# A hybrid encoder block on one core: attention's values taken one chunk later, and one list of other work over all pairs of heads

## The chip, the cores and the metric

The kernel runs on one core of a Trainium2 chip. The metric is device time in microseconds of one execution; shorter is better. A core has TensorE (PE; PEld is its weight load), VectorE (DVE), ScalarE (ACT), GpSimd (POOL) and SyncE (SP, which here issues nearly all DMAs). Each engine works through its own list of instructions in a fixed order and waits for others on semaphores.

## What is computed

One layer of an encoder block on 1024 positions of width 1024, with 16 learned meta positions put ahead (1040 in all). After an RMS norm, one input projection feeds two branches:

```
z = u @ w_in                          # u = RMSNorm(h)
rq, rk, rv, rg, aq, ak, av, ag, gr, ga = split(z)
branch A: bidirectional retention (4 heads), group norm, times silu(rg), @ w_rb
branch B: windowed attention (8 heads, 2 key groups), times silu(ag), @ w_ab
out = h + RMSNorm((sigmoid(gr) * A + sigmoid(ga) * B) @ w_o)
```

The attention works on blocks of 128 queries. A block sees its own 128 keys, those of the block before and the block after (within 128 positions), and the 16 meta keys; each head has a sink logit that takes part in the softmax:

```
s = concat(q . k_band, q . k_meta) * scale, masked
p = exp(s - m) / (sum(exp(s - m)) + exp(sink - m))
o = p_band @ v_band + p_meta @ v_meta
```

## The kernel before

All products are made to nearly full precision out of three rounded ones: each operand is split into a rounded high part (a copy, on ScalarE or GpSimd) and a low part (a subtraction on VectorE), and mm3 (lines 71 to 76) issues high x high, low x high and high x low. So every operand of a matmul costs a copy and a subtraction before TensorE can use it.

The stages follow each other. First the retention for four heads (lines 444 to 616), each with a forward and a backward scan over eight chunks; in the backward scan projections of the next head are put between the steps. After the fourth head come the projection of the attention's values (gen_av, lines 1246 to 1259, tile pav, copied to vraw) and the attention (lines 1261 to 1417). Then four large products, z, r, a and o (lines 1232 to 1237), run as seven products of blocks instead of eight; for these, sums of rows of x are made ahead (sum_fetch and sum_row, lines 689 to 705: load 2 x 512 KB, scale on ScalarE, four subtractions on VectorE, store to device memory), and some of the products of z too (gen_pre, lines 755 to 777, tile pe).

The attention handles pairs of heads hp = 0 to 3, with 8 chunks n of 128 queries each: 32 chunks. Pairs 0 and 1 use key group 0, pairs 2 and 3 group 1. A chunk has three stages:

- stage1 (lines 1274 to 1322): the scores of both heads (tile ps, three matmuls each), on VectorE the masked scores and their least value (raw, nm), on ScalarE the exponential with its sum (p, den), on VectorE the reciprocal, on GpSimd the scaling of p. It splits what it needs if that is not there yet: the queries (split_q, lines 635 to 641, tiles aqh and aql, from aq) and the values (vsplit, lines 1265 to 1272).
- stage2 (lines 1324 to 1356): TensorE transposes p into two banks (tile pt), ScalarE and VectorE split the result into pah and pal, pm, pbh and pbl.
- stage3 (lines 1358 to 1373): TensorE multiplies with the values (tile po, 7 or 10 matmuls), ScalarE copies to oa, and every second chunk SP stores oa.

The order is written out by hand in the loop of lines 1389 to 1417. For a chunk k it is: stage1 of k+1, stage2 of k, some steps of other work, stage3 of k. `follow` holds instructions behind those that it names, so that each engine's order comes out as written. The other work is a generator; one step is three matmuls, and FILL (line 26) says how many steps go into each chunk. It consists of projections of later queries (gen_aq, tile paq), keys of group 1 (gen_ak, tile pak) and early products of z (pe). Each pair of heads has its own list (fills, lines 1425 to 1433), and a new one begins when the pair ends. The weights for it (load_w, tiles wr, wh, wl; pre_fetch and pre_parts, tiles we, weh, wel) are loaded into two buffers of 512 KB that all loads share with the row sums; load_w issues the load and both splits together, with the high part on GpSimd. Keys of group 1 need the buffers of group 0, so between the pairs 1 and 2 the order is different: 16 steps ahead of the values of chunk (1, 7), and 16 more after the scores of (2, 0).

The row sums are made in the retention, one k for each head (lines 547 to 550). Three copies of rows of x to the output (x_to_out, lines 1419 to 1423) are issued after the first pair.

Of the kernel before, what the change touches and what calls it, by code (L numbers as in the profile page):

```python
# [25 lines left out]
FILL = (6, 5, 5, 5, 5, 5, 4, 5), (6, 5, 5, 6, 6, 6, 6, 16), (6, 5, 5, 5, 5, 5, 4, 5), (7, 7, 7, 7, 6, 6, 8)  # L26
# [12 lines left out]
def block_kernel(ctx: ExitStack, tc: tile.TileContext, xT, x, w_in, w_rb, w_ab, w_out, vecs, dec, sink,  # L39
# [62 lines left out]
    def load_w(src, u, act=False):  # L102
        hi, lo = [], []
        for s in range(2):
            raw = keep.tile([P, 4, 256], F32, tag="wr", bufs=2, name=f"wr{u}_{s}")
            nc.sync.dma_start(raw, src[u, :, 4 * s:4 * s + 4, :])
            h = wp.tile([P, 4, 256], R, tag="wh", bufs=4, name=f"wh{u}_{s}")
            l = wp.tile([P, 4, 256], R, tag="wl", bufs=4, name=f"wl{u}_{s}")
            if act:
                nc.scalar.copy(h, raw)  # L110
            else:
                pool_hi(h, raw)
            dve_lo(l, raw, h)
            hi.append(h)
            lo.append(l)
        return (lambda k, a, b: hi[k // 4][:, k % 4, a:b]), (lambda k, a, b: lo[k // 4][:, k % 4, a:b])

# [301 lines left out]
    vraw = va.tile([P, NB, 256], F32, name="vraw")  # L419
# [24 lines left out]
    def retention(h, fill):  # L444
# [199 lines left out]
    def load_aq(hp):  # L644
        wq[hp] = load_w(w_in, U_AQ + hp)

    def gen_aq(hp, i):
        if not i:
            if hp not in wq:
                load_aq(hp)  # L650
            aq[hp] = {}
        a, b = HALVES[i]
        for e_ in range(2):
# [4 lines left out]
            if hp or i:  # L658
                split_q(hp, e_, i)
# [5 lines left out]
    def load_ak():  # L665
        wak.append(load_w(w_in, U_AK))

    def gen_ak(g):
        if not wak:
            load_ak()  # L670
        kh, kl = (ra.tile([P, 4, 272], R, tag="kp", bufs=2, name=f"kT{s}{g}") for s in "hl")
        kT[g] = (kh, kl)
        for i, (a, b) in enumerate(PIECES):
            t = yield from proj(wak[0], P * g, a, b, f"pak{g}_{i}")
            o = ra.tile([P, 272], F32, tag="ak", bufs=2, name=f"akr{g}_{i}")
            rope_evac(t, a, b, o, f"ak{g}_{i}")
            s = NM if i == 0 else 0
            nc.scalar.copy(kh[:, i, 0:256], o[:, s:s + 256])
            dve_lo(kl[:, i, 0:256], o[:, s:s + 256], kh[:, i, 0:256])
            if i == 0:  # L680
                for j in range(4):
                    nc.scalar.copy(kh[:, j, 256:272], o[:, 0:NM])
                    dve_lo(kl[:, j, 256:272], o[:, 0:NM], kh[:, j, 256:272])
            yield
# [53 lines left out]
    def pre_parts(u):  # L738
# [4 lines left out]
        with follow(*softmax[-1:]):  # L743
            if n > P:
                v = t[:, :, P:n]
                g(v, raw[0][:, :, P:n], v, ALU.add)
                g(v, v, raw[0][:, :, 0:P], ALU.subtract)
                g(v, t[:, :, 0:P], v, ALU.subtract)
            h = wp.tile([P, 4, 256], R, tag="wh", bufs=4, name=f"weh{u}")[:, :, 0:n]
            l = wp.tile([P, 4, 256], R, tag="wl", bufs=4, name=f"wel{u}")[:, :, 0:n]  # L750
            nc.scalar.copy(h, t[:, :, 0:n])
            dve_lo(l, t[:, :, 0:n], h)
        parts[u] = h, l

    def gen_pre(u):
# [5 lines left out]
        ahead = 9 < u < 13  # L761
        if ahead:
            pre_fetch(u + 1)
        for p in PRE[u]:
# [10 lines left out]
            if ahead and p == 2:  # L775
                pre_parts(u + 1)
            yield

    def hooked(gen, at):

        for n, _ in enumerate(gen):
            for f, *a in at.get(n, ()):
                f(*a)
            yield
# [11 lines left out]
    scored, softmax, stored, values = [], [], [], {}  # L796
# [29 lines left out]
    last = "o", 3, 4  # L826
# [13 lines left out]
    class Phase:  # L840
# [65 lines left out]
        def product(self, u, p):  # L906
            if (self.nm, u, p) == last:
                return self.last_product(u, p)
            st = self.u.setdefault(u, {})
            at = {1: "X", 6: "X", 7: "W" if u in self.apart else "X", 5: "Y", 3: "V" if u in self.early or (self.nm, u) == last[:2] else "Y", 2: "Z",  # L910
# [26 lines left out]
        def combine(self, u, p, st):  # L937
# [28 lines left out]
            elif p == 6:  # L966
                copy("u2")
                if (self.nm, u) == last[:2]:
# [8 lines left out]
            elif p == 7 and not apart:  # L977
                copy("u3")
                if (self.nm, u) == last[:2]:
                    done("X")  # L980
            elif p == 3 and (self.nm, u) == last[:2]:
# [11 lines left out]
            if "u3" in st and "Y" in st and "c22" not in st:  # L993
                st["c22"] = plus(new("c5") if (self.nm, u) == last[:2] else st["u3"], st["u3"], "Y")
                self.post(u, 1, 1, st["c22"])
                if early or 3 in self.pre.get(u, ()) or (self.nm, u) == last[:2]:
# [246 lines left out]
    pm = [ap.tile([P, 256], R, name=f"pm{i}") for i in range(2)]  # L1243
    for t in (vm, pm[0], pm[1]):
        nc.vector.memset(t.bitcast(F32), 0.0)
    def gen_av():
        w = load_w(w_in, U_AV)
        for c in range(9):
# [7 lines left out]
            else:  # L1256
                nc.scalar.activation(vraw[:, c - 1], t[:, 0:256], AF.Copy, scale=rcol[:, c:c + 1])
            if c == NB - 1:
                yield

    def attention():
        oa, raw = [None], {}
        st1, st2 = {}, {}

        def vsplit(hp, b):
            g = hp // 2
            a_ = ap.tile([P, P], R, tag="vh", bufs=NB, name=f"vh{hp}_{b}")
            b_ = ap.tile([P, P], R, tag="vl", bufs=NB, name=f"vl{hp}_{b}")
            s = vraw[:, b, P * g:P * g + P]
            nc.scalar.copy(a_, s)  # L1270
            dve_lo(b_, s, a_)
            values[g, b] = (a_, b_)

        def stage1(hp, n):
# [14 lines left out]
            for b, _ in blocks:  # L1289
                if (g, b) not in values:  # L1290
                    vsplit(hp, b)
# [4 lines left out]
            for e_ in range(2):  # L1296
# [5 lines left out]
                scored.append(mm3(s[:, 0:wid], a_, b_, kh[:, start:start + wid], kl[:, start:start + wid], True, True))  # L1302
# [3 lines left out]
                p = ap.tile([P, 401], F32, tag="p", bufs=4, name=f"p{hd}_{n}")  # L1306
# [17 lines left out]
        def stage2(hp, n):  # L1324
# [33 lines left out]
        def stage3(hp, n):  # L1358
# [3 lines left out]
            for j, (b, h_, l_) in enumerate(bl):  # L1362
                mm3(po[:, 0:256], *values[g, b], h_, l_, j == 0, False)
# [13 lines left out]
        last = {}  # L1377

        def marks(*names):
            return [last[m] for m in names if m in last]  # L1380

        chunks = [(hp, n) for hp in range(4) for n in range(NB)]
        fill = filler(fills(0))[0]
        av = gen_av()
        next(av)
        stage1(0, 0)
        with follow(*latest):
            next(av, None)
        for (hp, n), follows in zip(chunks, chunks[1:] + [None]):
            if follows and follows != (2, 0):  # L1390
                with follow(*latest, *marks("oa", "lo")):
                    stage1(*follows)
            if (hp, n) == (3, NB - 2):
# [4 lines left out]
            with follow(*latest, *marks("exp", "sum")) if (hp, n) < (3, NB - 2) else ExitStack():  # L1398
                stage2(hp, n)
            if (hp, n) < (3, NB - 2):  # L1400
                if (hp, n) == (1, NB - 1):
                    fill = filler(fills(2))[0]
                with follow(*latest):
                    fill(FILL[hp][n])
            else:
                yield
            with follow(*latest) if (hp, n) < (3, NB - 2) else ExitStack():
                stage3(hp, n)
            if follows == (2, 0):
                with follow(*latest, *marks("oa", "lo")):  # L1410
                    stage1(2, 0)
                with follow(*latest):
                    fill(2 * KT)
            elif n == NB - 1 and hp < 3:
                fill = filler(fills(hp + 1))[0]
            if (hp, n) == (0, NB - 1):
                x_to_out()

    def x_to_out():

        with tc.issue_after(stored[0]):
            for r in (0, 4, 6):
                nc.sync.dma_start(out[P * r:P * r + 2 * P], x[P * r:P * r + 2 * P])

    def fills(hp):

        if hp == 1:
            return [hooked(gen_aq(1, 1), {5: [(pre_fetch, 8)], 11: [(pre_parts, 8)], 15: [(load_aq, 2)]}), pieces(pre, 8),
                    hooked(gen_aq(2, 0), {5: [(load_ak,)]})]
        if hp == 3:  # L1430
            return [hooked(gen_aq(3, 1), {3: [(pre_fetch, 10)], 9: [(pre_parts, 10)]}), pre]
        return [*([gen_ak(1)] if hp else []), hooked(gen_aq(hp, 1), {5: [(load_aq, hp + 1)]}),
                hooked(gen_aq(hp + 1, 0), {3: [(pre_fetch, 7 + hp)], 9: [(pre_parts, 7 + hp)]}), pieces(pre, 8)]
# [104 lines left out]
```

## Time and profile before

| | |
|---|---|
| runs of the kernel | 1137.64 us median of 3 (1137.25 to 1138.17) |
| the profiled execution's own time | 1137.18 us |
| its span in the profile | 1135.34 us |
| mean granted TensorE clock | 0.982 |
| first scores of the attention | at 363.2 us |
| scores of the second chunk | at 371.7 us |
| scores of the last chunk but one | at 614.4 us |
| first product of z | at 630.3 us |

A profile line of a group or of the timeline names the line in the kernel, engine, operation, output <- inputs and shape. In the timeline the first two columns are start and duration in us; in brackets stands how long the engine had been idle before, and what it waited for. Durations of matmuls overlap, since they are pipelined: what counts is the distance from one start to the next.

### The profile page before, as it was taken

What the parts mean: (1) busy time and instruction counts of PE and PEld (TensorE: products, weight loads), DVE (VectorE), ACT (ScalarE), POOL (GpSimd) and SP (SyncE); (2) the same over time, 40 slices, a digit from 0 to 9 for tenths busy, and PEclk for the clock granted to TensorE, in tenths of its full rate; (3) what the DMA queues carried; (4) which work ended last, traced back from release to release, by engine and by line L of the source; (5) the groups of instructions that cost most, each with busy time, mean ns of one, the idle gap of its engine ahead of it and who ended that gap; (6) DMA issues with size and microseconds to landing.
All of it is one profiled execution on the core that took longest, in us unless ns stands there. A gap on an engine that the chain in (4) does not pass through costs nothing.

```text
span 1135.3 us, 17083 instructions
## 1 busy us (share of the span) xinstructions
PE 1080.5 (95%) x5939; PEld 926.6 (82%) x5939; DVE 881.0 (78%) x1797; ACT 507.1 (45%) x1126; POOL 216.4 (19%) x276
## 2 busy tenths in 40 slices
PE   8999999899898899898899999999999999999997
PEld 7898889889887778697777778788888888787786
DVE  7887786877985665676666798999889979876775
ACT  7241432513423445434546664545546636433442
POOL 3323233243242322432220000000000000020032
PEclk9999999999999999899999999999999999999999
DMA  7140321411431411401124846999982763789563
GB/s 278 38 140 29 96 82 38 140 52 52 140 111 38 158 57 41 137 23 43 56 84 157 323 167 229 334 298 365 351 304 75 255 235 119 248 192 318 183 112 75
DMA packets 82903, 175.18 MB, mean 154 GB/s; under 512 B 8784, under 2 KB 22608, under 8 KB 82000
## 3 DMA queue, kind: packets, MB, share of 16 engines
q1 hardware_dynamic: 78928, 167.51, 42.9%
q0 software_dynamic: 3456, 6.29, 3.6%
q8 instruction: 47, 0.77, 0.3%
q10 hardware_dynamic: 432, 0.28, 0.1%
q14 instruction: 40, 0.33, 0.1%
HBM read 119.52 MB, written 57.67 MB: 156 GB/s over the span
## 4 chain that ended last, share of the span: by engine, by line
PE 74%; DVE 12%; DMA 7%; issue 3%; ACT 3%; POOL 1%; SPq 0%; DVEq 0%; POOLq 0%; ACTq 0%
PE bz L73 6%; PE bz L74 6%; PE bz L75 6%; PE pv L73 2%; PE br L74 2%; PE br L75 2%; PE br L73 2%; PE pv L74 2%; PE pv L75 2%; PE bo L73 2%; PE bo L74 2%; PE bo L75 2%; PE ba L74 2%; PE ba L73 2%; PE ba L75 2%
## 5 line engine op out<-in xcount | busy, mean ns | idle before, releaser
L1161 POOL DMA_DIRECT2D mx_d<-c1a x4 | 3.7, 920 | 405.8 <-DVE c1a L1152 405.8
L73 PE MATMUL bz<-T,lhz 128*128 128x512 f32 x192 | 75.6, 396 | 0.5 <-ACT u2z L943 0.4
L73 PE MATMUL pv<-wh,big 128*128 128x256 f32 x256 | 74.4, 291 | 1.6 <-DVE m_qk L174 1.3
L74 PE MATMUL bz<-T,llz 128*128 128x512 f32 x192 | 75.7, 395 | 0.0
L75 PE MATMUL bz<-T,lhz 128*128 128x512 f32 x192 | 75.6, 394 | 0.0
L74 PE MATMUL pv<-wh,big 128*128 128x256 f32 x256 | 73.6, 287 | 0.0
L75 PE MATMUL pv<-wl,big 128*128 128x256 f32 x256 | 73.3, 286 | 0.0
L73 PE MATMUL bz<-big,lhz 128*128 128x512 f32 x176 | 69.5, 397 | 1.2 <-ACT lhz L861 1.2
L74 PE MATMUL bz<-big,llz 128*128 128x512 f32 x176 | 69.7, 396 | 0.1
L75 PE MATMUL bz<-big,lhz 128*128 128x512 f32 x176 | 69.3, 394 | 0.0
L1307 DVE CUSTOM_DVE_ANT_0 raw<-ps,mask,nsink 128x400 f32<-128x400 f32 (+1 forms) x64 | 37.0, 598 | 34.6 <-PE ps L75 34.3
L1320 POOL TENSOR_SCALAR p<-p,den 128x400 f32<-128x400 f32 (+1 forms) x60 | 38.4, 654 | 130.4 <-DVE den L1313 113.4
L1310 ACT ACTIVATE p<-raw,nm 128x401 f32<-128x401 f32 (+1 forms) x64 | 38.4, 601 | 37.7 <-DVE nm L1307 37.5
L73 PE MATMUL paq<-big,wh 128*128 128x512 f32 x128 | 52.3, 409 | 0.0
L73 PEld LDWEIGHTS pv<-wh,big 128*128 128x128 f32 x256 | 49.2, 192 | 2.5 <-DVE m_qk L174 1.5
L74 PE MATMUL paq<-big,wl 128*128 128x512 f32 x128 | 50.6, 395 | 0.0
L75 PE MATMUL paq<-big,wh 128*128 128x512 f32 x128 | 50.4, 394 | 0.0
L74 PEld LDWEIGHTS pv<-wh,big 128*128 128x128 f32 x256 | 49.3, 193 | 0.1
L75 PEld LDWEIGHTS pv<-wl,big 128*128 128x128 f32 x256 | 49.2, 192 | 0.0
L89 DVE TENSOR_TENSOR wl<-wr,wh 128x1024 fp32r<-128x1024 f32 x28 | 37.3, 1335 | 15.3 <-POOL wh L86 15.1
L73 PEld LDWEIGHTS bz<-T,lhz 128*128 128x128 f32 x192 | 36.2, 188 | 9.7 <-ACT u2z L943 1.4
L75 PEld LDWEIGHTS bz<-T,lhz 128*128 128x128 f32 x192 | 36.2, 188 | 8.5
(631 smaller groups left out, 3651.0 us busy)
## 6 DMA issues: line engine op xcount, KB each, us to landing
wrz<-in_w_in_dram SPq DMA_DIRECT2D x32, 512.0 KB, 5.7
wr<-in_w_in_dram SPq DMA_DIRECT2D x29, 512.0 KB, 3.7
e<-e SPq DMA_DIRECT2D x40, 256.0 KB, 3.8
we<-in_w_in_dram SPq DMA_DIRECT2D x16, 512.0 KB, 3.7
tg<-tg_d SPq DMA_DIRECT2D x32, 256.0 KB, 4.9
T<-preT SPq DMA_DIRECT2D x6, 1024.0 KB, 7.1
xs<-in_xT_dram SPq DMA_DIRECT2D x8, 512.0 KB, 3.5
xsT<-xs SPq DMA_DIRECT2D x16, 256.0 KB, 2.1
```

The costliest lines, as they stand in the source:

```text
L73: nc.tensor.matmul(o, ah, bh, start=first, stop=False, **kw)
L74: nc.tensor.matmul(o, al, bh, start=False, stop=False, **kw)
L75: latest[:] = [nc.tensor.matmul(o, ah, bl, start=False, stop=last, **kw).ins]
L89: return nc.vector.tensor_tensor(o, i, hi.bitcast(F32), ALU.subtract).ins
L1161: nc.gpsimd.dma_start(d, to, accum_op=ALU.add)
L1307: nc.vector.tensor_tensor_reduce(raw[e_][:, 1:1 + wid], s[:, 0:wid], mask[:, mo:mo + wid], -SCALE, nsink[:, hd:hd + 1], ALU.add, ALU.min, ...
L1310: last["exp"] = nc.scalar.activation(p[:, 0:1 + wid], raw[e_][:, 0:1 + wid], AF.Exp, scale=-1.0, bias=nm_[:, e_:e_ + 1], accum_out=den[:, ...
L1320: nc.gpsimd.tensor_scalar(pt[e_][:, 0:wid], pt[e_][:, 0:wid], den[:, e_:e_ + 1], 1.0, op0=ALU.mult, op1=ALU.mult)
```

## The change

Four things are done, all in the attention and what feeds it.

1. *Order of a chunk.* After: stage1 of k+1, stage2 of k, steps of other work, stage3 of k-1. The last chunk's stage3 comes at the end. pbh and pbl get two buffers instead of one. The exception between pairs 1 and 2 is gone.
2. *Values.* vsplit is gone. gen_av writes the high part from the bank itself (vah, ScalarE) and the low part too (val, VectorE, reading the bank a second time). The first scores come one projection chunk earlier in the program, behind the latest matmul.
3. *Other work.* One list over all pairs, in which keys of group 1 alternate with queries of pair 2, and FILL is set anew (200 steps in all, as before). Loads, splits and row sums are taken out of the generators and put at numbered steps (BEGUN), behind the last exponential and reciprocal. Query splits are made there as well. The weight splits of queries and keys in the attention have their high part on ScalarE instead of GpSimd. Keys of group 1 are rotated into a buffer first and split by `keys`.
4. *Moves.* The row sums go from the retention into this list. x_to_out comes after chunk 13 (pair 1, chunk 5) instead of after pair 0. One of the two buffers of p for each pair of chunks is taken from the queries' pool of six.

The core of the diff:

```diff
-FILL = (6, 5, 5, 5, 5, 5, 4, 5), (6, 5, 5, 6, 6, 6, 6, 16), (6, 5, 5, 5, 5, 5, 4, 5), (7, 7, 7, 7, 6, 6, 8)
+FILL = (8, 8, 6, 7, 6, 6, 7, 6), (6, 7, 6, 6, 7, 6, 6, 7), (7, 8, 8, 6, 6, 6, 7, 7), (6, 6, 5, 5, 5, 5, 8)
...
-                sum_fetch(h)
-            if c == 3:
-                with follow(state["v"], state["vl"]):
-                    sum_row(h)
...
+    def parts_aq(hp):
+        wq[hp] = split_w(wq[hp], U_AQ + hp, True)
...
+    def keys(g, i):
+
+        if not i:
+            kT[g] = [ra.tile([P, 4, 272], R, tag="kp", bufs=2, name=f"kT{s}{g}") for s in "hl"]
+        kh, kl = kT[g]
+        o = rotated_k.pop((g, i))
+        s = NM if i == 0 else 0
+        nc.scalar.copy(kh[:, i, 0:256], o[:, s:s + 256])
+        dve_lo(kl[:, i, 0:256], o[:, s:s + 256], kh[:, i, 0:256])
...
+    def hooked(gens, at):
+
+        n = 0
+        for g in gens:
+            for _ in g:
+                with follow(*marks("exp", "sum")):
+                    for f, *a in at.get(n, ()):
+                        f(*a)
+                n += 1
+                yield
...
-                nc.scalar.activation(vraw[:, c - 1], t[:, 0:256], AF.Copy, scale=rcol[:, c:c + 1])
+                nc.scalar.activation(vah[:, c - 1], t[:, 0:256], AF.Copy, scale=rcol[:, c:c + 1])
+                nc.vector.scalar_tensor_tensor(val[:, c - 1], t[:, 0:256], rcol[:, c:c + 1],
+                                               vah[:, c - 1].bitcast(F32), op0=ALU.mult, op1=ALU.subtract)
...
-                bh_ = ap.tile([P, 256], R, tag="pbh", bufs=1, name=f"pbh{hp}_{n}")
-                bl_ = ap.tile([P, 256], R, tag="pbl", bufs=1, name=f"pbl{hp}_{n}")
+                bh_ = ap.tile([P, 256], R, tag="pbh", bufs=2, name=f"pbh{hp}_{n}")
+                bl_ = ap.tile([P, 256], R, tag="pbl", bufs=2, name=f"pbl{hp}_{n}")
...
+        fill = filler([hooked([gen_aq(0, 1), pieces(pre, 8), gen_aq(1, 0), gen_aq(1, 1), pieces(pre, 8), gen_aq(2, 0),
+                               gen_ak(1, (0, 1)), gen_aq(2, 1, (0,)), gen_ak(1, (2,)), gen_aq(2, 1, (1,)),
+                               gen_ak(1, (3,)), gen_aq(3, 0), gen_aq(3, 1), pre], BEGUN)])[0]
...
+            if k + 1 < len(chunks):
+                with follow(*latest, *marks("oa", "lo")):
+                    stage1(*chunks[k + 1])
+                if chunks[k + 1] == (1, NB - 1):
+                    keys(1, 0)
...
+            with follow(*latest, *marks("exp", "sum")) if not ends else ExitStack():
                 stage2(hp, n)
...
+            if not ends:
                 with follow(*latest):
                     fill(FILL[hp][n])
...
+            with follow(*latest) if not ends else ExitStack():
+                if k:
+                    stage3(*chunks[k - 1])
...
+    BEGUN = {0: [(pre_fetch, 7)], 6: [(pre_parts, 7)], 7: [(fetch_aq, 1)], 12: [(split_q, 0, 0, 1)],
+             16: [(parts_aq, 1)], 18: [(sum_fetch, 0)], 20: [(split_q, 0, 1, 1)], 28: [(sum_row, 0)],
+             30: [(pre_fetch, 8)], 36: [(split_q, 1, 0, 0)], 38: [(pre_parts, 8)], 40: [(fetch_aq, 2)],
...
+             180: [(pre_fetch, 13)], 188: [(pre_parts, 13)]}
```

More of the change, by code (lines that the diff above doesn't have):

```diff
@@ L742, in pre_parts @@
         t = raw[-1]
[L743 to L752, printed above, removed]
+        if n > P:
+            v = t[:, :, P:n]
+            g(v, raw[0][:, :, P:n], v, ALU.add)
+            g(v, v, raw[0][:, :, 0:P], ALU.subtract)
+            g(v, t[:, :, 0:P], v, ALU.subtract)
+        h = wp.tile([P, 4, 256], R, tag="wh", bufs=4, name=f"weh{u}")[:, :, 0:n]
+        l = wp.tile([P, 4, 256], R, tag="wl", bufs=4, name=f"wel{u}")[:, :, 0:n]
+        nc.scalar.copy(h, t[:, :, 0:n])
+        dve_lo(l, t[:, :, 0:n], h)
         parts[u] = h, l
@@ L795, in block_kernel, with marks @@
     pre, fetched_w, parts = all_pre(), {}, {}
-    scored, softmax, stored, values = [], [], [], {}
+    softmax, stored, last = [], [], {}
+    def marks(*names):
+        return [last[m] for m in names if m in last]
     with tc.issue_after(normed):
@@ L967, in combine @@
                 copy("u2")
[L968 removed]
+                if (self.nm, u) == final[:2]:
                     plus(st["u2"], st["u2"], "Y")
@@ L1406, in attention @@
+            if ends:
                 yield
[L1407 to L1416, printed above, removed]
-                x_to_out()
+            if k == 13:
+                x_to_out()
```

147 lines of the change are left out of this document (62 added, 85 removed).

## The prediction

> **What bounds the kernel now.** I read the page first: its span, the engines' busy shares and the chain that ended last.
>
> ```profile
> span 1135.3 us, 17083 instructions
> ...
> PE 1080.5 (95%) x5939; PEld 926.6 (82%) x5939; DVE 881.0 (78%) x1797; ACT 507.1 (45%) x1126; POOL 216.4 (19%) x276
> ...
> PE 74%; DVE 12%; DMA 7%; issue 3%; ACT 3%; POOL 1%; SPq 0%; DVEq 0%; POOLq 0%; ACTq 0%
> ```
>
> TensorE is the bound, and every matmul of the kernel before is still there after: its order lists the same 5870 rows. So only time in which TensorE stood still or ran slowly can change. The view of busy time by stage says where that is. Its columns are busy time of each engine with instructions in brackets, granted TensorE clock, DMA share, GB/s.
>
> ```profile
> 333.00:371.60 38.60, 33.67 (x258) 32.32 (x257) 24.16 (x72) 12.42 (x35) 10.67 (x18) 0.91 0.09 28
> 371.60:614.30 242.70, 219.50 (x1221) 189.11 (x1221) 157.78 (x354) 113.54 (x305) 69.68 (x83) 0.96 0.25 83
> ...
> 650.00:1135.00 485.00, 477.23 (x2059) 385.02 (x2057) 407.67 (x681) 237.01 (x432) 27.03 (x32) 1.00 0.71 228
> ```
>
> After 650 TensorE is full at full clock, and the change doesn't touch it. From the second chunk's scores (371.6) to those of the last chunk but one (614.3), 29 chunks of attention, it is busy 219.5 of 242.7 us at a clock of 0.96. The idle part is 23.2 us. The slow clock cost 219.5 x 0.04 = 8.8 us. Together **32.0 us** could be had; 210.7 us is the floor of this stretch, and it is the same after, since the changed kernel has 187 steps of other work in these chunks where the kernel before had 186. What TensorE waited for there, from the view of waits (total us, times, longest):
>
> ```profile
> PE po L75 <- DVE pbl L89: 9.9, 6, 2.2
> PE ps L73 <- ACT aqh L639: 7.1, 3, 2.5
> PE po L73 <- ACT pbh L1353: 3.3, 5, 0.9
> PE po L75 <- DVE pal L89: 1.4, 3, 0.6
> PE ps L74 <- DVE aql L89: 1.2, 2, 0.9
> ```
>
> That is 22.9 of the 23.2 us, and it has two causes. In 14.6 us the values' product (po) waits for its own chunk's split probabilities; in 8.3 us the scores (ps) wait for a split of queries that is made on demand. One chunk in the timeline shows the first:
>
> ```profile
> 440.93 0.60 PE L1330 MATMUL pt<-ident,p 128*128 128x128 f32 x4
> ...
> 441.72 0.48 PE L73 MATMUL paq<-big,wh 128*128 128x512 f32 x1
> ...
> 443.01 1.18 POOL L1320 TENSOR_SCALAR p<-p,den 128x400 f32<-128x400 f32 x2 [5.55 <-DVE den L1313]
> ...
> 445.15 0.69 DVE L174 TENSOR_TENSOR m_aq<-paq,sr 64x512 f32<-64x512 f32 x1
> 445.27 0.28 PE L73 MATMUL po<-pah,vh 128*128 128x256 f32 x1
> ...
> 445.88 0.41 DVE L89 TENSOR_TENSOR pm<-pt,pm 16x256 fp32r<-16x256 f32 x1
> ...
> 446.32 0.37 ACT L1353 CAST pbh<-pt 128x256 fp32r<-128x256 f32 x1 [2.56 <-DVE pm L89]
> ...
> 446.75 0.38 PE L73 MATMUL po<-pbh,vh 128*128 128x256 f32 x1 [0.61 <-ACT pbh L1353]
> ...
> 448.66 0.60 PE L1330 MATMUL pt<-ident,p 128*128 128x128 f32 x4
> ```
>
> Transposes at 440.9, five steps of projection (15 matmuls in 3.55 us, 0.71 a step), then po, which needs pbh. The split of pbh stood behind VectorE's rotation of queries (m_aq), so TensorE waited. With other work in the queue the wait is 2.2 us.
>
> **The change part by part.**
>
> *Values one chunk behind.* The changed kernel's TensorE order is: scores of chunk k+1, transposes of k, the steps, values of k-1. So pal, pbh and pbl get a whole chunk (some 7 us) more, where the longest wait was 2.2. The 14.6 us go. Next in line is the scaled p that the following transposes need. Here p was done 443.01 + 1.18 = 444.19, 3.3 us after the scores' end at 440.93; the next transposes came at 448.66, 4.5 us later. With 6.4 steps a chunk instead of 5 the gap grows. So p may come 4 us late before TensorE feels it. The doubled buffers of pbh and pbl keep the older pair alive; the values' bank is free a chunk early. Nothing is added on the path.
>
> *Queries' splits at fixed steps.* The 8.3 us go, less what comes late by its place. Two places look tight. Step 20 splits for scores that come after step 22, and on ScalarE it stands behind two weight splits of 1.05 us (row below), which use up its lead and some more: 0.7 us late, an estimate. The second group's keys may overwrite the first's only after the last score of head pair 1, and ScalarE takes these copies ahead of pbh, which the next transposes' bank waits for: 1.2 us, an estimate from four short operations of 0.3 us or so each.
>
> *The one list with its loads and row sums.* It moves work onto engines that have room, if it has. The prices, from the grouped rows:
>
> ```profile
> L704 DVE TENSOR_TENSOR xs<-xs x8: 673/710/887, 55.9 to 286.9; 128x512 f32<-128x512 f32 x8
> ...
> L700 ACT ACTIVATE xs<-xs,vec x8: 1137/1148/1156, 54.7 to 280.7; 128x1024 f32<-128x1024 f32 x8
> ```
>
> ```profile
> L751 ACT CAST weh<-we 128x1024 fp32r<-128x1024 f32 x6 | 6.3, 1048 | 8.7 <-DVE we L748 8.7
> ```
>
> VectorE takes 16 row subtractions, 16 x 0.71 = 11.4 us, on top of 157.8: 169 of about 215 us, less the values' splits, which now happen at the projection. ScalarE takes 8 x 1.15 + 8 x 1.05 (weights, formerly GpSimd's) = 17.6 on 113.5: 131 of 215. Both fit on the mean, and GpSimd, which scales p, loses the weight splits. Counting the order chunk by chunk, the fullest is VectorE's around the last chunk of pair 2: 9.3 us of work against TensorE's 8.0. That is 1.3 late, inside the margin of 4. I leave 2.6 us for such places. If the cover failed, the whole 11.4 + 17.6 = 29 us would be the price. So this stretch: -32.0 + 0.7 + 1.2 + 2.6 = **-27.5 us** (bounds: -32, and -3 with the cover gone).
>
> *Loads.* Fifteen loads now start 6 to 18 steps ahead of their split, each behind the split that frees its two buffers. A landing takes
>
> ```profile
> we<-in_w_in_dram SPq DMA_DIRECT2D x14, 512.0 KB, 3.6
> ```
>
> 3.6 us; six steps are 6 x 215/187 = 6.9. Hidden. On SP each load waits for the split that frees its buffers, and behind it stand the stores of oa and of the early products; their buffers are used again two or more chunks later, so such a wait reaches nobody unless it lasts that long. The three copies of x to the output start six chunks later, beside a DMA share of 0.25: nothing.
>
> *Retention without row sums.* There the waits from 120 to 302 show weights that come late, since the sums held their buffers:
>
> ```profile
> PE pak L73 <- POOL wh L86: 2.2, 2, 1.6
> PE pkv L73 <- ACT kvb L535: 1.8, 3, 0.9
> PE pk L73 <- DVE vl L89: 1.6, 1, 1.6
> ```
>
> 2.2 + 1.6 should go (vl stood behind a weight split); the new order of the rest is open, so I take **-3** (bounds -8 and +2).
>
> *The values' projection.* VectorE now reads its bank a second time (val, 8 of them, about 0.48 us by the row of op below, which reads as much from a bank), and its order puts the first three behind the whole backward scan. So only 88 projection matmuls instead of 184 fill the scan, and its last passes lack cover:
>
> ```profile
> 351.38 0.28 PE L73 MATMUL pb<-Shb,qh 128*128 128x256 f32 x1
> ...
> 356.80 0.28 PE L73 MATMUL pav<-wh,big 128*128 128x256 f32 x1
> ...
> 357.87 0.28 PE L73 MATMUL pav<-wh,big 128*128 128x256 f32 x1
> 357.98 0.28 PE L73 MATMUL pb<-Shb,qh 128*128 128x256 f32 x1
> ...
> 361.21 0.41 PE L571 MATMUL to<-ident,op 128*128 128x128 f32 x2 [0.44 <-DVE op L603]
> 363.24 0.91 PE L73 MATMUL ps<-kTh,aqh 128*128 128x272 f32 x2 [1.62 <-ACT aqh L639]
> 365.83 0.59 PE L74 MATMUL ps<-kTh,aql 128*128 128x272 f32 x1 [1.68 <-DVE aql L89]
> ```
>
> ```profile
> 345.36 0.48 DVE L595 SCALAR_TENSOR_TENSOR op<-pb,qd,op 128x256 f32<-128x256 f32 x1 [1.10 <-PE pb L75]
> ...
> 347.15 0.40 DVE L603 TENSOR_SCALAR op<-op,mv,rs 128x256 f32<-128x256 f32 x1
> ```
>
> A pass took (357.98 - 351.38) / 2 = 3.3 us under its filler; VectorE's part is 345.36 to 347.55, 2.2. So three bare passes are shorter by about 1 us each, and the scan starts about 2.6 us sooner (22 matmuls fewer ahead of it): the last transpose comes near 355.4 instead of 361.2. Then 120 matmuls at 0.119 (from 356.80 to 357.87 are nine), 14.3 us, the first scores 0.8, a first wait for val of 1.1, and about 2 for a slow clock after the gaps: second scores at 373.5 instead of 371.6. The 3.3 us of waits in the last two rows go, and are in that count. **+2** (bounds -1 and +6).
>
> The sum: -27.5 - 3 + 2 = -28.5 us. The profiled execution took 1137.18 us, 1.84 beyond its span, and is 0.46 under the median of the runs, 1137.64. 1137.2 - 28.5 = **1109 us**.
>
> **The rivals.**
>
> *The slow clock stays.* Of my 32 us, 8.8 are clock.
>
> ```profile
> 411.00:417.00 6.00, 5.32 (x23) 4.77 (x24) 4.42 (x11) 4.59 (x11) 1.93 (x3) 0.72 0.29 89
> ```
>
> ```profile
> 411.68 0.39 PE L75 MATMUL po<-pbl,vh 128*128 128x256 f32 x1 [2.17 <-DVE pbl L89]
> ```
>
> Here the clock falls to 0.72 right after an idle gap of 2.17 us, which speaks for gaps as its cause. If they are not, the clock stays at 0.96: 1109 + 8 = 1117. [...] Chance 0.13.
>
> *New waits take part of it back.* Splits and sums crowd VectorE and ScalarE in places where I counted margin; with half of the 27.5 lost, 1123. Chance 0.12.
>
> *Loads decide: slower.* The splits now sit at fixed places in ScalarE's queue, ahead of pbh and the next exponentials. If a load lands late, these stand behind it.
>
> ```profile
>   POOL wh L86: 20.7, 7
> ```
>
> In retention GpSimd waited 20.7 / 7 = 3.0 us for a load. The margin is 6.9 - 3.6 = 3.3 us; 15 loads each later than 3.3 + 28.5 / 15 = 5.2 us would eat the gain; at 6 us each the time is 1109 + 15 x 2.7 = 1149. Against it: most loads have 8 steps and more. Chance 0.08.
>
> *Nothing happens*, within 0.2% (about what a measurement can tell from no change): the order shows the move as described, so 0.02.
>
> **How the numbers follow.** Forecast 1109, its own range 1100 to 1118: 0.55. Better, 1093 to 1100 (retention's bound and no new waits): 0.10. The rest as above. The range that holds 8 in 10 is 1093 to 1128. Faster 0.55 + 0.10 + 0.13 + 0.12 = 0.90, same 0.02, slower 0.08.
>
> **What would show it.** Right: no wait of po on pbl, pbh or pal; ps waiting under 2 us in all; a clock of 0.99 or more in the attention; chunks of 6 to 8 us. Wrong: transposes waiting on p's scaling, ScalarE's xs or wh waiting on DMA, a scan whose last passes are longer than 3 us, or second scores later than 378 less what retention gained.

## The result, and the profile after

The changed kernel takes 1090.58 us (median of 4 runs, 1090.21 to 1091.09) against 1137.80 us before: a ratio of 0.9586, 95% interval 0.9569 to 0.9602. The forecast was 1109 with a range of 1093 to 1128. So the direction was right, and the time lies 2.4 us under the range. The profiled execution took 1090.71 us, with this page:

```profile
span 1088.9 us, 17108 instructions
...
PE 1060.2 (97%) x5939; PEld 914.8 (84%) x5939; DVE 878.6 (81%) x1789; ACT 510.1 (47%) x1118; POOL 209.8 (19%) x268
...
PE 81%; DVE 9%; DMA 6%; issue 2%; ACT 2%; POOL 0%; SPq 0%; DVEq 0%; POOLq 0%; ACTq 0%
```

TensorE's share of the chain that ended last went from 74 to 81%. VectorE's busy time is nearly the same: nothing was saved there, only moved.

To see where the 46.4 us of span went, I cut both traces at the same events of TensorE.

| event | before, us | after, us | this part's gain |
|---|---|---|---|
| second chunk's scores | 371.7 | 355.9 | -15.8 |
| scores of the last chunk but one | 614.4 | 569.8 | -28.8 |
| first product of z | 630.3 | 586.7 | +1.0 |
| end of the span | 1135.3 | 1088.9 | -2.8 |

The attention (29 chunks) gave what was forecast for it, 28.8 against 27.5. What comes ahead of it gave 15.8, where the forecast had 3 less 2, so 1. That is the miss: 14.8 of the 18.4 us between 1109 and 1090.6. Busy time by stage (columns as above) for the kernel before, up to the first matmul of the values' projection:

```profile
0.00:333.00 333.00, 315.78 (x2237) 292.74 (x2238) 265.71 (x644) 121.09 (x305) 109.01 (x143) 0.98 0.30 102
```

and for the changed kernel, for that stage, the scan's tail with the values' projection, and the attention:

```profile
0.00:318.00 318.00, 308.56 (x2242) 288.40 (x2243) 257.45 (x631) 114.19 (x298) 110.31 (x144) 1.00 0.24 80
318.00:355.80 37.80, 34.71 (x253) 32.18 (x251) 23.11 (x73) 11.37 (x31) 9.11 (x16) 0.86 0.09 29
355.80:569.80 214.00, 206.01 (x1216) 181.04 (x1215) 164.03 (x356) 124.90 (x307) 63.29 (x76) 1.00 0.39 132
```

In the first stage TensorE's idle time fell from 17.2 to 9.4 us and its clock rose from 0.98 to 1.00. In the attention the idle time is 8.0 us instead of 23.2, at a clock of 1.00 instead of 0.96, though VectorE does 164 us of work there instead of 158. What TensorE still waits for in the attention:

```profile
PE ps L74 <- DVE aql L89: 3.4, 2, 2.4
PE pt L1344 <- DVE pbl L89: 2.8, 4, 1.0
PE pt L1341 <- DVE pal L89: 1.3, 1, 1.3
PE ps L73 <- ACT aqh L642: 0.5, 1, 0.5
```

No wait of po is left. One chunk in the timeline shows why:

```profile
430.17 1.19 POOL L1331 TENSOR_SCALAR p<-p,den 128x400 f32<-128x400 f32 x2 [4.50 <-DVE den L1324]
...
431.71 0.28 PE L73 MATMUL po<-pah,vah 128*128 128x256 f32 x1
...
432.01 0.38 ACT L1364 CAST pbh<-pt 128x256 fp32r<-128x256 f32 x1
...
432.42 0.42 DVE L89 TENSOR_TENSOR pbl<-pt,pbh 128x256 fp32r<-128x256 f32 x1
...
433.64 0.60 PE L1341 MATMUL pt<-ident,p 128*128 128x128 f32 x4
```

po at 431.71 starts ahead of this chunk's pbh (432.01) and pbl (432.42): it works on the pair of the chunk before. p's scaling ends at 431.36, 2.3 us ahead of the transposes that need it.

And the view of waits for the retention. Before:

```profile
POOL wh L86 <- DMA wr<-in_w_in_dram: 33.8, 12, 4.7
...
PE tr L478 <- ACT ost L576: 1.5, 3, 0.6
PE pk L74 <- DVE wl L89: 1.4, 2, 1.1
PE to L571 <- DVE op L603: 1.1, 1, 1.1
```

After:

```profile
POOL wh L86 <- DMA wr<-in_w_in_dram: 1.8, 1, 1.8
PE pb L73 <- DVE op L598: 1.2, 1, 1.2
```

Before, GpSimd waited 33.8 us in 12 places for weights to land. After, it waits once. The prediction's own row of 20.7 us in 7 waits was a piece of this, and it was read only as the price of a load.

### The profile page after: what moved, and what is told of

It reads as the page before. It is cut to its first block, busy times and chain, and to the rows that moved or that the text cites. A ratio compares the mean times of both kernels' runs of the same rounds, so it can differ in the third digit from the quotient of the medians.

```text
span 1088.9 us, 17108 instructions
## 1 busy us (share of the span) xinstructions
PE 1060.2 (97%) x5939; PEld 914.8 (84%) x5939; DVE 878.6 (81%) x1789; ACT 510.1 (47%) x1118; POOL 209.8 (19%) x268
## 4 chain that ended last, share of the span: by engine, by line
PE 81%; DVE 9%; DMA 6%; issue 2%; ACT 2%; POOL 0%; SPq 0%; DVEq 0%; POOLq 0%; ACTq 0%
PE bz L73 6%; PE bz L74 6%; PE bz L75 6%; PE pv L73 3%; PE pv L74 2%; PE pv L75 2%; PE br L74 2%; PE br L75 2%; PE br L73 2%; PE bo L74 2%; PE bo L73 2%; PE bo L75 2%; PE ba L74 2%; PE paq L74 2%; PE ba L75 2%
## 5 line engine op out<-in xcount | busy, mean ns | idle before, releaser
L73 PEld LDWEIGHTS pv<-wh,big 128*128 128x128 f32 x256 | 48.2, 188 | 1.7 <-DVE m_qk L181 1.5
L74 PEld LDWEIGHTS pv<-wh,big 128*128 128x128 f32 x256 | 48.2, 188 | 0.2
L74 PEld LDWEIGHTS bz<-T,llz 128*128 128x128 f32 x192 | 36.2, 188 | 8.4
```

The source lines that it names most:

```text
L73: nc.tensor.matmul(o, ah, bh, start=first, stop=False, **kw)
L74: nc.tensor.matmul(o, al, bh, start=False, stop=False, **kw)
```

## The experiments

Ratios are against the kernel before on the same chip.

### The row sums put back into the retention

```diff
                 while pend:
                     pend.pop(0)()
+                sum_fetch(h)
+            if c == 3:
+                with follow(state["v"], state["vl"]):
+                    sum_row(h)
...
-             16: [(parts_aq, 1)], 18: [(sum_fetch, 0)], 20: [(split_q, 0, 1, 1)], 28: [(sum_row, 0)],
+             16: [(parts_aq, 1)], 20: [(split_q, 0, 1, 1)],
```

(and so for the other three)

> The changed kernel with the row sums back in the retention (fetch at c = 1, row at c = 3 of each head) and out of the attention's list. Theory: the retention's 14 us were the row sums', which held the two shared weight buffers and filled VectorE; then first scores come near 363 instead of 349.5, and the time is 1103 to 1106 (1091 + 12 to 15). Rival: the row sums cost what the prediction gave them, 3 us, and the rest came from another order of the retention: 1092 to 1095. The attention's stretch stays within 3 us of 214 either way.

Measured: 1104.77 us (1102.61 to 1105.91), ratio 0.971 [0.9677, 0.9743]. Second scores at 368.0 us, 12.1 later than in the changed kernel; the attention's stretch is nearly the same, 213.0. So the row sums cost 12 to 14 us where they were. Where they are now they cost little, though more than the 0.9 us by which the stretch is longer with them. In this kernel's profile the clock fell to 0.74 (506 to 512 us) after a gap of 2.39 us at step 124, and that chunk took 12.4 us. The changed kernel has the same gap, kept its clock at 1.00 and took 10.8. Without that difference of 1.6 us the sums cost some 2.5 us there, of which 2.0 are waits (8.0 us against 6.0). The retention of this kernel by stage, and in the timeline where the sums of the second head are made:

```profile
46.00:315.00 269.00, 258.74 (x1926) 242.14 (x1925) 218.52 (x557) 95.50 (x274) 89.31 (x124) 1.00 0.26 85
```

```profile
128.30 2.19 ACT L721 ACTIVATE xs<-xs,vec 128x1024 f32<-128x1024 f32 x2
...
132.60 0.68 DVE L725 TENSOR_TENSOR xs<-xs,xs 128x512 f32<-128x512 f32 x1
...
133.79 0.68 DVE L725 TENSOR_TENSOR xs<-xs 128x512 f32<-128x512 f32 x1
134.24 0.43 SPq L105 DMA_DIRECT2D wr<-in_w_in_dram  x1
...
134.77 0.39 SPq L726 DMA_DIRECT2D xsT<-xs  x1
...
138.98 1.05 POOL L86 TENSOR_SCALAR wh<-wr 128x1024 fp32r<-128x1024 f32 x1 [4.24 <-DMA wr<-in_w_in_dram]
139.60 0.33 SPq L105 DMA_DIRECT2D wr<-in_w_in_dram  x1
140.06 1.22 DVE L89 TENSOR_TENSOR wl<-wr,wh 128x1024 fp32r<-128x1024 f32 x1 [1.56 <-POOL wh L86]
141.20 0.42 DVE L89 TENSOR_TENSOR vl<-pv,vh 128x256 fp32r<-128x256 f32 x1
141.76 0.37 PE L73 MATMUL pk<-big,wh 128*128 128x272 f32 x1 [1.82 <-DVE vl L89]
```

Here is the whole chain, to be read downwards. The scalings start at 128.30 and the four subtractions end at 134.5. The third of them (132.60) is the last of them to use the first buffer, and that buffer's load of weights is issued at 134.24. The fourth (133.79) and its store (134.77) hold the second buffer, whose load is issued at 139.60. GpSimd stands 4.24 us for the first, VectorE 1.56 us for GpSimd's high part, and behind it in VectorE's queue stands vl, which has nothing to do with weights and for which TensorE waits 1.82 us. So a buffer that is held too long showed at TensorE as a wait for something else.

### The same with buffers of their own for the row sums

```diff
+        xb = va.tile([P, NB, 256], F32, tag="vah", bufs=1, name=f"xb{k}")
         for i in range(2):
-            t = keep.tile([P, 4, 256], F32, tag="wr", bufs=2, name=f"xs{i}{k}").rearrange("p a b -> p (a b)")
+            t = xb[:, 4 * i:4 * i + 4].rearrange("p a b -> p (a b)")
```

> The kernel of e1_sums_back (the changed kernel with the row sums still in the retention), with one difference: the row sums have 1 MB of their own there (the memory that later holds the values' high part) instead of the two buffers that all weight loads share. Theory (the row sums cost the retention time because they hold the weights' buffers, so that weights and their splits come late, and the clock falls after those gaps): the waits of TensorE on wl, wh and vl (5.6 us in e1_sums_back) go; second scores at 357 to 361 us instead of 368.0, total 1094 to 1099 against 1104.8. Rival (the sums' own work is in the way: 16 subtractions of 0.71 us on VectorE, 8 scalings of 1.15 us on ScalarE): second scores stay at 366 to 368, total 1102 to 1105.

Measured: 1094.96 us (1093.59 to 1095.42), ratio 0.9619 [0.9587, 0.965]; second scores at 360.0. Waits of the retention:

```profile
POOL wh L86 <- DMA wr<-in_w_in_dram: 9.8, 4, 4.8
...
PE tr L484 <- ACT ost L582: 1.8, 3, 0.6
```

GpSimd's wait for loads fell from 35.4 us (12 waits, in the kernel above) to 9.8 with the same bytes moved (87 GB/s against 85 in 46 to 315 us). So it is not the traffic. The buffers account for 8.0 of the 12.1 us. Some 4 us stay. The waits name 1.3 of them (tr waits 1.8 us for ScalarE's ost, 0.5 in the changed kernel); that they come from the sums' own place in the queues is argued, not shown.

### The same without the sums' arithmetic

```diff
-            nc.scalar.activation(t, t, AF.Copy, scale=vec[:, 4 * i + k:4 * i + k + 1])
...
-            nc.vector.tensor_tensor(x[o], x[a], x[b], ALU.subtract)
             nc.sync.dma_start(xs_d[n][k], x[o])
```

> The kernel of e1_sums_back with the 8 scalings and 16 subtractions of the row sums left out: rows of x are loaded into the shared buffers and stored as they are, so the sums are not computed. Theory (buffers): the loads still hold the two shared buffers, if for a shorter time, since nothing is computed between landing and store; most of the loss stays: second scores at 363 to 368, total 1099 to 1105. Rival (arithmetic): second scores at 356 to 359, total 1092 to 1096.

Measured: 1089.56 us (1087.76 to 1090.9), ratio 0.9574 [0.9547, 0.9602]; second scores at 357.4. My theory's number (1099 to 1105) is missed; the second scores came where the rival had them, and the total lies under both. Without the arithmetic 10.6 of the 12.1 us come back though the buffers are shared as before, because they are then held only for a load and a store:

```profile
POOL wh L86 <- DMA wr<-in_w_in_dram: 6.9, 3, 3.7
```

So "buffers" and "arithmetic" are no rivals: they are the two ends of one chain. The arithmetic, slow in full queues, is what holds the buffers. Breaking it at either end frees the weights (8.0 and 10.6 of 12.1).

### Values' product of the same chunk

```diff
-                if k:
-                    stage3(*chunks[k - 1])
+                stage3(hp, n)
...
-        stage3(*chunks[-1])
```

> The changed kernel with the values' product of chunk k again behind the steps of chunk k, all else as changed. Theory: the delay is what removed 14.6 us of idle time and about two thirds of 8.8 us of slow clock, so 1091 + 15 to 20 = 1106 to 1111. Rival: the longer filling (6.4 steps a chunk instead of 5) and a VectorE order without query splits ahead of pbh would have been enough: 1091 + 0 to 6.

Measured: 1109.13 us (1107.19 to 1110.22), ratio 0.9754 [0.9716, 0.9791]; attention's stretch 232.2, 18.3 longer. The waits of po are back, with more steps in each chunk than before the change:

```profile
PE po L75 <- DVE pbl L89: 10.7, 7, 2.7
PE po L73 <- ACT pbh L1364: 3.9, 2, 2.4
```

So the delay by one chunk is what removes them; more cover alone doesn't.

### Query splits on demand

```diff
-    BEGUN = {0: [(pre_fetch, 7)], 6: [(pre_parts, 7)], 7: [(fetch_aq, 1)], 12: [(split_q, 0, 0, 1)],
-             16: [(parts_aq, 1)], 18: [(sum_fetch, 0)], 20: [(split_q, 0, 1, 1)], 28: [(sum_row, 0)],
...
+    BEGUN = {0: [(pre_fetch, 7)], 6: [(pre_parts, 7)], 7: [(fetch_aq, 1)], 16: [(parts_aq, 1)], 18: [(sum_fetch, 0)], 28: [(sum_row, 0)],
```

(all split_q out of the list of fixed steps)

> The changed kernel with no query split at fixed steps; each is made when its scores ask for it. Theory: 8.3 us of idle time and a third of the slow clock come back, less the 3.9 us that the changed kernel still waits for aqh and aql: 1091 + 5 to 10 = 1096 to 1101. Rival: with values one chunk behind TensorE has work to bridge a split, so within 3 us of 1091.

Measured: 1113.78 us (1112.95 to 1115.93), ratio 0.9794 [0.9761, 0.9827]; attention's stretch 237.3, 23.4 longer. The direction is as expected, the size more than twice. The waits and the stage:

```profile
PE ps L74 <- DVE aql L89: 7.0, 5, 2.1
PE ps L73 <- ACT aqh L642: 5.1, 5, 1.2
```

```profile
357.10:594.40 237.30, 219.94 (x1215) 188.77 (x1214) 167.85 (x356) 125.53 (x307) 62.75 (x76) 0.96 0.35 119
```

12.1 us of waits on queries come in pairs, one for the high part and one for the low part, and the clock goes back to 0.96. TensorE's idle time is 9.4 us more than in the changed kernel and its busy time 13.9 us more; of these 13.9 the clock explains 219.94 x 0.04 = 8.8, and the rest stays open. I had priced the slow clock at a third of that. The run shows what splits on demand cost in the new order. It does not show what the kernel before paid, since that kernel made most of its splits behind their projections (see below).

### The row sums moved in the kernel before

```diff
-                sum_fetch(h)
...
-                    sum_row(h)
...
-                    hooked(gen_aq(2, 0), {5: [(load_ak,)]})]
+                    hooked(gen_aq(2, 0), {0: [(sum_fetch, 1)], 4: [(sum_row, 1)], 7: [(load_ak,)]})]
...
-            return [hooked(gen_aq(3, 1), {3: [(pre_fetch, 10)], 9: [(pre_parts, 10)]}), pre]
+            return [hooked(gen_aq(3, 1), {3: [(pre_fetch, 10)], 9: [(pre_parts, 10)], 11: [(sum_fetch, 3)], 15: [(sum_row, 3)]}), pre]
```

(and the other two in the same way: the row sums go into the fill lists, at steps between the loads that are there)

> The kernel before with one part of the change alone: its row sums moved from the retention into the attention's lists of other work. Theory: the retention gives 12 to 15 us, and the crowded attention takes back 0 to 6: 1138 - 6 to 15 = 1123 to 1132. Rival (the prediction's sizes): 1134 to 1138.

Measured: 1145.14 us (1141.72 to 1146.3), ratio 1.0059 [1.004, 1.0079]. It is 0.6% slower, which no theory had. The retention did gain: second scores at 353.6 instead of 371.7, 18.1 us. But the attention's stretch went from 242.7 to 265.7:

```profile
PE po L75 <- DVE pbl L89: 10.8, 9, 2.2
PE ps L73 <- ACT aqh L635: 7.8, 3, 2.9
PE pe L73 <- ACT weh L747: 7.4, 1, 7.4
```

```profile
353.60:619.40 265.80, 227.16 (x1222) 194.02 (x1221) 168.97 (x371) 121.63 (x313) 71.44 (x83) 0.92 0.32 107
```

With po still waiting in its own chunk, its waits come to 21.8 us instead of 14.6, a load behind the sums' buffers is late once (weh, 7.4 us), and the clock is 0.92. So the parts of the change are not additive: in the whole change the sums cost some 2.5 us in the attention, alone 23. That po waits in its own chunk accounts for a part of this; which part of the change keeps the loads on time no run separates.

### High parts of the weights on GpSimd again

```diff
-        wq[hp] = split_w(wq[hp], U_AQ + hp, True)
+        wq[hp] = split_w(wq[hp], U_AQ + hp)
```

(and for the keys)

> The changed kernel with the high parts of the weight splits in the attention back on GpSimd (1.16 us each) instead of ScalarE (1.04 us each), 8 of them. Theory (this part of the change is worth little: p's scaling on GpSimd has a margin of some 4 us): 1090 to 1093. Rival (p's scaling stands behind two splits of 1.16 us and the transposes wait): 4 to 8 us more, 1094 to 1099, with waits of pt on p.

Measured: 1089.14 us (1088.81 to 1089.95), ratio 0.9573 [0.9547, 0.9598], no difference that can be told from the changed kernel. So no gain of this part by itself is shown.

### Splits in halves

```diff
-             16: [(parts_aq, 1)], 18: [(sum_fetch, 0)], 20: [(split_q, 0, 1, 1)], 28: [(sum_row, 0)],
+             14: [(half_aq, 1)], 17: [(parts_aq, 1)], 18: [(sum_fetch, 0)], 20: [(split_q, 0, 1, 1)],
+             26: [(sum_row, 0)], 28: [(sum_rest, 0, SUMS[2:])],
```

(and so for the other weights and sums)

> The changed kernel with VectorE's load in the attention spread: the two halves of a weight split (about 1.2 us each on VectorE) at two steps some 3 to 7 steps apart instead of one, row sums in two pairs of subtractions instead of four at once, the weights of queries of pair 3 loaded three steps earlier. Theory (what TensorE still waits for in the attention, 8.0 us, comes from single chunks in which VectorE has more work than TensorE): the waits on aql and pbl at steps 20, 68 and 124 go, 4 to 7 us; attention stretch 207 to 210 instead of 213.9, total 1083 to 1087. Rival (the waits move to the next chunk, since VectorE's mean is already 164 of 214 us): 1089 to 1092.

Measured: 1089.67 us (1088.57 to 1090.78), ratio 0.9576 [0.955, 0.9603]; stretch 213.4. The rival holds: waits of 6.2 us in all, some of them in other chunks.

```profile
PE pt L1362 <- DVE pbl L89: 2.6, 3, 1.8
PE ps L74 <- DVE aql L89: 2.2, 1, 2.2
```

The wait on aql stayed, since one half still stood ahead of that query split on VectorE.

### Spare matmuls behind the scan

```diff
+    def spare(c, behind, n=4):
+        o = p2(f"spare{c}")
+        z = xm.rearrange("p k e -> p (k e)")
+        with tc.issue_after(behind):
+            for i in range(n):
+                behind = nc.tensor.matmul(o, z[:, 0:P], z, start=True, stop=True).ins
...
+            if h == NH - 1 and c < 5:
+                spare(c, passed)
```

(and two each behind three of the transposes `to`)

> The changed kernel with 22 matmuls of 128x512 more, whose result nobody reads (on data that lies ready, into a bank of their own), put behind the last passes of the last head's backward scan, where in the changed kernel TensorE stands still for 0.5 to 1 us at a time (330 to 338 us) and the clock is 0.50 until 343. They are 5.2 us of TensorE work at full clock that the reference doesn't need. Theory (the clock falls when TensorE has too little to do over a few us, also without a gap above 1 us): clock 0.95 or more from 330 to 346, the 72 matmuls of the values' projection behind the scan run at 0.117 us apart from their start, second scores at 352 to 355 instead of 355.9, total 1087 to 1090. Rival (the clock has another cause, or the spare matmuls delay the scan by what they save): clock still 0.5 there, second scores at 357 to 361, total 1091 to 1096.

Measured: 1090.84 us (1090.19 to 1094.01), ratio 0.9592 [0.9564, 0.9621]; second scores at 353.2. The changed kernel's tail by stage:

```profile
330.00:338.00 8.00, 5.01 (x23) 3.09 (x22) 6.63 (x24) 3.06 (x10) 3.40 (x7) 0.70 0.20 66
338.00:346.00 8.00, 7.90 (x45) 7.53 (x46) 3.38 (x10) 2.67 (x7) 0.00 (x0) 0.66 0.21 68
```

The same with the spare matmuls:

```profile
330.00:338.00 8.00, 7.68 (x43) 5.89 (x41) 7.30 (x26) 3.34 (x12) 3.27 (x6) 1.00 0.21 69
338.00:346.00 8.00, 7.85 (x66) 7.85 (x67) 3.18 (x9) 2.48 (x6) 0.00 (x0) 1.00 0.19 64
```

The clock stays at 1.00, and from 338 to 346 TensorE gets through 66 matmul records instead of 45. So it is what TensorE lacks in these few us that lowers the clock here, as the theory says. Whether that is the busy share, the many short gaps or the share of transposes in what is left, this run doesn't separate, since the spare matmuls change all three. The 2.7 us gained up to the second scores did not reach the total: the stretch behind was 1.9 us longer in this profile. In it the clock fell after the gap of 2.39 us at step 124: the four transposes next behind it took 1.06 us, against 0.60 in the changed kernel. Over the 16 us around the gap TensorE was busy 13.11 us at 0.89, so an estimate of 13.11 x 0.11 = 1.4 of the 1.9 us. The changed kernel's profile has the same gap and keeps its clock:

```profile
494.00:510.00 16.00, 13.10 (x76) 11.12 (x75) 11.05 (x23) 8.95 (x23) 4.13 (x5) 1.00 0.28 83
```

```profile
492.00:508.00 16.00, 13.11 (x68) 11.01 (x67) 9.34 (x20) 7.23 (x20) 2.93 (x3) 0.89 0.26 83
```

(first the changed kernel, then the one with spare matmuls)

### The two together, with the gap at step 124 made smaller

```diff
-             106: [(fetch_aq, 3)], 108: [(split_q, 2, 0, 1)], 116: [(keys, 1, 2)], 120: [(parts_aq, 3)],
-             124: [(sum_fetch, 3), (split_q, 2, 1, 1)], 132: [(keys, 1, 3)], 134: [(sum_row, 3)],
+             103: [(fetch_aq, 3)], 108: [(split_q, 2, 0, 1)], 113: [(half_aq, 3)], 116: [(keys, 1, 2)],
+             122: [(split_q, 2, 1, 1)], 125: [(parts_aq, 3)], 126: [(sum_fetch, 3)], 132: [(keys, 1, 3)], 134: [(sum_row, 3)],
```

> The kernel of e10_spare_matmuls with the high parts of the weight splits on GpSimd (as in e9_high_parts_on_gpsimd), the weights of pair 3 loaded 3 steps earlier and split in two halves, at step 113 and at step 125, and the query split of step 124 at step 122, between them. Theory (the gap of 2.39 us at step 124 comes from two weight splits ahead of that query split on VectorE, and it draws the clock drop that took e10's gain away): the gap is 1.2 us or less, no chunk longer than 10 us, attention stretch 210 to 213, total 1085 to 1088. Rival (the halves only move the wait): a gap of 2 us or more somewhere else, stretch 214 to 216, total 1089 to 1092.

Measured: 1086.47 us (1085.89 to 1088.33), ratio 0.9545 [0.9524, 0.9566], faster than the kernel before and, by some 0.4%, than the changed kernel (0.9569 to 0.9602). Stretch and total are as expected, and the longest chunk is 9.3 us. The gap is 1.7 us, more than the 1.2 that I gave it, and the clock holds over it:

```profile
355.10:565.90 210.80, 205.88 (x1215) 180.96 (x1214) 162.80 (x356) 117.56 (x299) 78.74 (x84) 1.00 0.40 134
```

In this profile the second scores come at 355.1, not at 353.2 as in the kernel above. The tail kept its gain (19.3 us from the last pass of the scan to the second scores in both, 21.5 in the changed kernel), but the first 46 us ran at a clock of 0.96 instead of 1.00, which no part of the change touches.

## Why the prediction was right in the attention and wrong ahead of it

*Values one chunk behind: right.* It put 14.6 us of waits there; all are gone, and undoing this part alone costs 18.3 us.

*Query splits at fixed steps: the waits went, but their cause was misread.* The term was 8.3 us for splits "made on demand". In the kernel before, gen_aq makes each split right behind its projection, all but those of pair 0's first half. The three long waits stand where the projection itself ends just ahead of the scores that need it:

```profile
391.65 0.39 PE L75 MATMUL paq<-big,wh 128*128 128x512 f32 x1
...
394.26 1.26 POOL L175 TENSOR_TENSOR aq<-m_aq,m_aq 128x512 f32<-128x512 f32 x1 [3.12 <-DVE m_aq L174]
...
395.56 0.62 ACT L639 CAST aqh<-aq 128x512 fp32r<-128x512 f32 x1
...
396.23 0.45 PE L73 MATMUL ps<-kTh,aqh 128*128 128x400 f32 x1 [2.46 <-ACT aqh L639]
```

Rotation and split take from 392.1 to 396.2, and TensorE waits for the last 2.5 us of them. The new FILL also ends this projection earlier: for pair 0 it is done 6 steps ahead of these scores, where it was done right ahead of them. How much of the 8.3 us went by that and how much by the fixed steps is not shown.

*The stretch: -28.8 against -27.5, but by two errors that nearly cancel.* Waits left over are 8.0 us instead of the 4.5 allowed (0.7 + 1.2 + 2.6). At step 20 it is 1.0 (forecast 0.7). At the second group's keys it is 2.1 (forecast 1.2), with the sums' subtractions ahead of pal on VectorE as the larger cause. Step 124, 2.9 us, was in no term. The floor of 210.7 us was too high: 213.9 - 8.0 = 205.9. Two digits of the clock explain at most 219.5 x 0.005 = 1.1 of these 4.8 us. A further part may lie in how busy time is counted: a matmul ahead of a gap counts with its whole duration (0.39 us, where starts are 0.23 apart), and there were 19 waits before and 8 after, so an estimate of 11 x 0.16 = 1.8 us. The rest stays open. No wait of po and a clock of 1.00 came as said. Three other signs did not: ps waited 3.9 us where under 2 was said, chunks took 5.0 to 10.8 us instead of 6 to 8, and the weight load of the transposes waited once for p (1.5 us, in the gap at the second group's keys).

*Row sums in the attention: right.* VectorE does 164 us of work there, against 154 with the sums in the retention. That costs the 0.9 us of the stretch, or some 2.5 with the difference of the clock, inside the 2.6 that the prediction left for such places. Loads hidden: right too, with 2.0 us of waits on DMA in the whole stretch, both on engines that had room.

*Retention without row sums, -3 with a bound of -8: the step that failed.* The mechanism (weights come late since the sums held their buffers) was right, and the size was not. The runs give 12.1 us in the changed kernel and 18.1 in the kernel before. Three things made the term too small. It counted two waits, 2.2 and 1.6, where TensorE's waits from 46 us on are 10.5 us (2.3 after). The others have names that don't speak of weights (kvb, ost, op, vl). They went with the sums all the same; that vl stood behind a late weight split is shown above, for the others it is inferred. Its window began at 120 and so left out the first head, though that held only 1.1 of the 10.5. And it left out the slow clock. In the kernel before that cost, by its rows from 200 to 240 and from 280 to 315,

```profile
200.00:240.00 40.00, 37.12 (x276) 34.96 (x276) 34.03 (x93) 18.82 (x54) 10.94 (x17) 0.96 0.32 108
...
280.00:315.00 35.00, 31.64 (x239) 30.15 (x238) 32.17 (x82) 16.47 (x49) 10.44 (x13) 0.95 0.40 128
```

37.1 x 0.04 + 31.6 x 0.05 = 3.1 us, which the kernel with the sums put back, at a clock of 1.00 in both, did not pay in its profile. The same reading, busy time and clock by stage, that gave 32 us in the attention would have given 17.2 + 315.8 x 0.02 = 23.5 us ahead of it as the most that could be had. The bound of -8 had nothing to do with that number. Of the 12.1 us the named waits make about 8; the rest I can't assign. Not all of the 15.8 and 18.1 us are the sums': 1.3 and 1.5 us were there at the scan's first matmul (tr, at 48.2 us in the kernel before). The kernel before ran its first 46 us at a clock of 0.96 in its profile; the two kernels that it is compared with here ran them at 1.00, and so did the one with the sums put back (tr at 47.0).

*Values' projection, +2: right in sign, its size less sure.* The kernel before with its sums moved reaches its second scores at 353.6, the changed kernel at 355.9: +2.3. The other pair has the sums in the retention in both, and there it is 371.7 and 368.0: -3.7. Of these the slow clock of the kernel before, which the other did not have, makes 1.3 + 3.1 = 4.4 us; without it +0.7. The 2 us of slow clock in this term came as said: behind the scan some 20 matmuls start 0.21 us apart instead of 0.117.

*The end: 0, measured -1.8 (+1.0 and -2.8).* About 1 us of the latter is idle time; the rest stays open.

*The rivals.* "The slow clock stays" fell: with 8.0 us of idle time instead of 23.2 the clock is 1.00, and it came back to 0.96 with 17.4 us of idle time in the kernel that splits queries on demand. "New waits take part back": only the 3.5 us above. "Loads decide" did not occur in the change; the moved sums in the kernel before show that it can (weh, 7.4 us).

## What to carry to other kernels

Where a stage has idle time and a slow clock, take its whole loss (idle time plus busy time at the missing clock) as the measure of what an edit there may give (in the attention it was 4.8 us short); the named waits of the bound engine are only the last link, and the waits of the engines that feed it on their loads show the first (in the retention before 10.5 us of TensorE's against 33.8 of GpSimd's for weights). A buffer shared between loads and a slow side computation is paid by whatever is loaded next (here 12.1 us, of which buffers of their own gave back 8.0). Room comes first: here moving side work paid only together with the rest of the change, and alone it made the kernel 0.6% slower.

## What the runs showed of the hardware

The granted clock fell without a long gap. In the tail of the changed kernel's scan no gap was above 1.0 us, TensorE was busy 5.0 of 8 us, and the clock went to 0.70 and 0.66 over 16 us (two stages shown above); filled with matmuls whose result nobody reads it stayed at 1.00. So here the longest gap alone doesn't tell the clock: in this one execution a gap of 1.0 us went with 0.66, and one of 2.39 us with 1.00.

Whether one gap of 2.39 us lowers the clock differs between executions in which that place has the same order (1.00 in the changed kernel and 0.89 with the spare matmuls, over the 16 us around it). What makes the difference is not shown. The spread of the kernel before goes with the clock too: its runs beside these experiments go from 1133.0 us at a mean clock of 0.987 to 1143.4 at 0.976.
